# First four FFN groups begin with the two block products that need half of the tokens; output tiles written as their sums are complete

## The chip, the cores and the metric
One core of a Trainium2 chip runs one transformer block. The time is the device time of one execution in microseconds (us). The kernel before takes 2693.76 us, the median of 3 runs (2691.06 to 2694.64). One further execution was profiled: 2691.3 us, with a span of 2689.6 us from its first to its last instruction.

## The reference
The block has 512 tokens of width 2048, all in float32. Two attention branches are added to x; then the FFN follows, and it is the part that the change touches:

```
x  = x + gt1 * (merged @ w_out)
h2 = _rms(x, g_norm2) * (1 + sc2) + sh2          # the norm needs a token's whole row
gate, up = jnp.split(h2 @ w_ffn_in, 2, axis=-1)  # 2048 -> 2 x 5632
x  = x + gt2 * ((jax.nn.silu(gate) * up) @ w_ffn_out)
```

## The kernel before
**Engines.** TensorE (PE) multiplies and transposes, ScalarE (ACT) casts and applies functions, VectorE (DVE) adds and scales, SP issues the loads from memory in program order, and GpSimd (POOL) issues the stores to scratch memory and most of the output. Channels lie on the 128 partitions, tokens along the free axis.

**Three products for one.** float32 is multiplied as three products of a rounded high part and a low part: hi x lo, hi x hi, lo x hi. So each weight block is loaded raw (`raw`, 512 KB), ACT casts it to `whi`, and DVE subtracts to make `wlo`. Inputs are split in the same way (`x`, `x12h`, `x12l`).

**Seven block products.** The FFN's first matrix is worked through in 11 groups (FG) of 4 + 4 tiles of 128 columns. Within a group the product is a 2 x 2 block product: tokens in two halves (th = 0, 1), the 2048 input channels in two halves, columns in two (gate and up). Instead of 8 block products a Strassen–Winograd scheme makes 7, from sums of blocks: P1, P5, P7, P3, P6, P2, P4 in this order (lines from 1168, `PROD`). P1 is X11·W11 and P2 is X12·W21: both need the first half of the tokens alone. P5, P7, P3 and P6 need sums over both halves (`x12`, `x34`, made in `x_sums`), P4 the second half. A product is 4 pieces of 12 matmuls (128x512), 48 in all. A piece takes one weight block, or, where the scheme wants a difference of weights, a block into which DVE has subtracted another (`raw<-raw,raw`).

**Pieces and buffers.** `ahead_to(i, 2, 6)` keeps the pieces made (whi, wlo) 2 ahead and their loads issued 6 ahead; there are 10 raw buffers, 3 of whi and 3 of wlo. A block is dropped after the last product that uses it (`LAST`). PSUM has 3 buffers of the tag mm, 2 of s, 2 of t and 1 of y; P1 and P2 sum into s, s; P5 and P3 into t, t; P7 and P4 into mm, mm; P6 into mm, y. PE works in program order here, DVE and ACT in the order of a scheduler.

**Norm.** `norm2(k, th)` scales and shifts channel tile k for one half of the tokens, and splits it. It needs that half's rstd: `last_sum(th)` makes it from the sum of squares and puts it on a diagonal (`diag`), `last_row(th)` spreads it by a matmul. The first half's k < 8 are made first; then P1 of group 0 runs, with `last_sum(1)` and `last_row(1)` in it; all that remains (`second_norms`: first half's k ≥ 8, second half, sums) is issued at piece 3 of group 0, before P5.

**After the products.** `act_back1` and `act_back2` transpose a group's result back on PE, split it and park it in scratch memory by POOL's queue (`apark`). `act_back2(g-1)` runs after P1 of group g.

**FFN output and end.** The second matrix goes in 5 chunks of groups (CH), each for 2 column halves q, with the same seven products, summed in SBUF (`acc`). After P4 of the last chunk, `out_tiles(q, col_)` (lines 1470 to 1487) loads the residual (`xo<-xpark`), transposes the sums in PSUM tiles of tags mm and y, scales and adds on DVE and stores the tile; column half 1 first, then 0.

Of the kernel before, what the change touches and what calls it, by code (L numbers as in the profile page):

```python
# [9 lines left out]
F32 = mybir.dt.float32  # L10
# [77 lines left out]
def kernel(  # L88
# [40 lines left out]
    def t2(name, dtype=F32, w=T):  # L129
        return tp.tile([P, w], dtype, tag="t2", name=nm(name))  # L130
# [46 lines left out]
    def sync_dma(dst, src):  # L177
        tc.keep_in_program_order(nc.sync.dma_start(dst, src))
# [982 lines left out]
    def kmc(key, ap):  # L1161
# [6 lines left out]
    PROD = {  # L1168
        "P1": ((1, 1), "11", None), "P5": (1, "12", "11"), "P7": (3, "22", "12"), "P3": (4, "22", None),
        "P6": (2, "22", "11"), "P2": ((1, 2), "21", None), "P4": ((2, 2), "21", "22"),  # L1170
    }

    INTO = {"P5": "11", "P7": "12", "P6": "22", "P4": "21"}
    LAST = {"P7": ("12",), "P6": ("11",), "P4": ("21", "22")}

    def piece_keys(stage, g, prod, j):
        _, x, y = PROD[prod]
# [28 lines left out]
    def add_do(fn):  # L1206
        ev.append((None, fn))
# [32 lines left out]
        return [ps(t) for t in tags]  # L1240


    def ffn_in_group(g, order):
        G = {}
        n = KD // 4

        def product(prod, bank, start, stop):
            def use(w, j):
                if j == 0 and start:
                    G[bank] = tb(*{"A": ("s", "s"), "B": ("t", "t"), "C": ("mm", "mm"), "D": ("mm", "y")}[bank])  # L1250
                for kk in range(2):
                    prod_mm(G[bank], X[PROD[prod][0], 2 * j + kk], w, kk, start and j == 0 and kk == 0,
                            stop and j == n - 1 and kk == 1)
            for j in range(n):
                add_piece(("a", g, prod, j), lambda w, j=j: use(w, j))

        def both(fn):
            add_do(lambda: [fn(t) for t in range(2)])

        def copy_to(name, bank):  # L1260
            def fn(t):
                G[name, t] = t2(name)
                act.copy(G[name, t], G[bank][t])
            both(fn)

        def add_bank(name, bank, out=None):
            def fn(t):
                dst = G[name, t] if out is None else t2(out)
                vec.tensor_tensor(dst, G[name, t], G[bank][t], ALU.add)
                G[out or name, t] = dst  # L1270
            both(fn)

        def after_p6(t):
            u, z = G["u", t], G["z", t]
            vec.tensor_tensor(z, z, u, ALU.add)
            c12 = t2("c12")
            vec.tensor_tensor(c12, u, G["B"][t], ALU.add)
            G["c12", t] = c12

        def after_p2(t):  # L1280
            s = t2("silu")
            act.activation(s, G["A"][t], AF.Silu)
            vec.tensor_tensor(s, s, G["c12", t], ALU.mult)
            G["a1", t] = s
            G["c12", t] = None

        def after_p4(t):
            u = G["u", t]
            vec.tensor_tensor(u, u, G["C"][t], ALU.add)
            act.activation(u, u, AF.Silu)  # L1290
            vec.tensor_tensor(u, u, G["z", t], ALU.mult)
            G["a2", t] = u
            G["z", t] = None

        product("P1", "A", True, False)
        copy_to("p1", "A")
        if g > 0:
            add_do(lambda: act_back2(g - 1))
        product("P5", "B", True, False)
        copy_to("z", "B")  # L1300
        product("P7", "C", True, False)
        add_bank("z", "C")
        product("P3", "B", False, True)
        product("P6", "D", True, True)

        def u_of(t):
            vec.tensor_tensor(G["p1", t], G["p1", t], G["D"][t], ALU.add)
            G["u", t] = G.pop(("p1", t))
        both(u_of)
        both(after_p6)  # L1310
        product("P2", "A", False, True)
        both(after_p2)
        product("P4", "C", False, True)
        both(after_p4)
        add_do(lambda: act_back1(g))
        groups[g] = G

    groups = {}
    apark = [dp.tile([P, 7 * T], F32, name=f"apark_{i}") for i in range(2 * FG)]
    yraw = {}  # L1320

# [45 lines left out]
            park(2 * g + j, 5, split_t(s34, "y34"))  # L1367


    def first_norms():  # L1370
        for k in range(8):
            norm2(k, 0)
    add_do(first_norms)
    ffn_in_group(0, None)

    def at_product(n, fn):

        i = next(i for i, e in enumerate(ev) if e[0] == n)
# [5 lines left out]
    def second_norms():
        for k in range(8):
            norm2(k + 8, 0)
            norm2(k, 1)
            norm2(k + 8, 1)
            x_sums(k)
    at_product(3, second_norms)  # L1390
    for g in range(1, FG):
        ffn_in_group(g, None)


    CH = ((0, 1, 2), (3, 4), (5, 6), (7, 8), (9, 10))
# [17 lines left out]
    def ffn_out_chunk(ci, q):  # L1413
        B = {}
        gs = CH[ci]
        final = ci == len(CH) - 1

        def evac(prod):
            for t in range(2):
                bank = B[BANK[prod]][t]  # L1420
                if ci == 0:
                    a = t2("acc")
                    act.copy(a, bank)
                    acc[q, prod, t] = a
                else:
                    a = acc[q, prod, t]
                    vec.tensor_tensor(a, a, bank, ALU.add)
                if final:
                    finish(q, prod, t)

        for prod in ORDER:
            start = prod in ("P1", "P5", "P7", "P6")
            if ci == 0 and q == 0:
                add_do(lambda prod=prod: y_load(0, prod))
            for gi, g in enumerate(gs):
                def use(w, prod=prod, gi=gi, g=g, start=start):
                    b = BANK[prod]
                    if gi == 0 and start:
                        B[b] = tb(*TAGS[b])
                    for kk in range(2):  # L1440
                        y = Y[g, kk, prod]
                        prod_mm(B[b], (y[:, 0:256], y[:, 256:512]), w, kk, start and gi == 0 and kk == 0,
                                gi == len(gs) - 1 and kk == 1)
                        if q == 1:
                            del Y[g, kk, prod]
                add_piece(("b", (q, g), prod, 0), use)
            add_do(lambda prod=prod: evac(prod))
            if prod == "P1" and ci == q == 0:
                add_do(lambda: act_back2(FG - 1))
            if q == 1 and ci + 1 < len(CH):  # L1450
                add_do(lambda prod=prod: y_load(ci + 1, prod))

    def finish(q, prod, t):
        get = lambda n: acc[q, n, t]
        if prod == "P6":
            u = get("P6")
            vec.tensor_tensor(u, u, get("P1"), ALU.add)
            z = get("P5")
            vec.tensor_tensor(z, z, get("P7"), ALU.add)
            vec.tensor_tensor(z, z, u, ALU.add)  # L1460
            c12 = get("P3")
            vec.tensor_tensor(c12, c12, u, ALU.add)
            fin[q, 2, 2, t], fin[q, 1, 2, t] = z, c12
        if prod == "P2":
            fin[q, 1, 1, t] = get("P2")
        if prod == "P4":
            c = get("P4")
            vec.tensor_tensor(c, c, get("P6"), ALU.add)
            fin[q, 2, 1, t] = c

    def out_tiles(q, col_):
        xr_ = {}
# [24 lines left out]

# [95 lines left out]
```

## Time and profile before

| | us |
|---|---|
| median of 3 runs | 2693.76 (2691.06 to 2694.64) |
| profiled execution, its own time | 2691.3 |
| its span | 2689.6 |
| PE, DVE, ACT, POOL busy | 2584.3, 2024.8, 1149.4, 154.9 |
| mean granted PE clock | 0.985 of full speed |

Busy time counts what an engine executes, without waiting. A stretch of the span is read in a table of windows: its length, then for each engine the busy time and how many instructions it ran, then the granted clock of PE (1.00 is 2.4 GHz, half of it is 1.2 GHz), the share of time in which the DMA engines were busy, and what they moved. A group of instructions is read as: engine, operation, output<-inputs, shapes, number | busy time, mean ns of one | idle time just before, and what ended it. Names such as `ps_t` are the program's tiles without their numbers. Line L82 is that of a helper which records nearly all operations, so tiles tell more than lines.

### The profile page before, as it was taken

Reading aid. Unit: us, or ns where it says so; the run is one execution under the profiler, and the core shown is the slowest. Engines: PE = TensorE matmul, PEld = TensorE weight load, DVE = VectorE, ACT = ScalarE, POOL = GpSimd, SP = SyncE. Lnnn points to the kernel's source line nnn. Section 1 sums busy time; section 2 is a strip of 40 time slices with the busy share of each in tenths; the row PEclk is TensorE's granted clock in tenths of the full one; section 3 lists DMA queues with packets and bytes.
Section 4 is the critical chain, followed back from the end, with each engine's and each line's share of the span. In section 5 each row is a group of like instructions: output and inputs, shape, how many; then the busy total and the mean of one; then the engine's idle time right before and its main releaser. Section 6 shows DMA issues by size and latency. Waiting matters only on the chain.

```text
span 2689.6 us, 32101 instructions
## 1 busy us (share of the span) xinstructions
PE 2584.3 (96%) x12166; PEld 2147.2 (80%) x12166; DVE 2024.8 (75%) x2614; ACT 1149.4 (43%) x1557; POOL 154.9 (6%) x256
## 2 busy tenths in 40 slices
PE   6999999999999999999779999999999999999997
PEld 4788888888899888888558888888888887888885
DVE  8966766657877854533768888888888887689997
ACT  4434655542333322222545544455544445543331
POOL 0000000000110100000001100111110111000001
PEclk9999999999999999999879999999999999999998
DMA  9854444336666783332325445445444549765562
GB/s 341 300 195 164 160 150 143 128 134 235 252 248 251 263 347 141 141 141 98 94 63 167 144 136 160 158 144 172 151 136 151 164 135 327 235 210 193 189 206 79
DMA packets 236579, 487.29 MB, mean 181 GB/s; under 512 B 15428, under 2 KB 159044, under 8 KB 211336
## 3 DMA queue, kind: packets, MB, share of 16 engines
q1 hardware_dynamic: 215552, 426.03, 46.5%
q0 software_dynamic: 14816, 48.51, 5.0%
q10 hardware_dynamic: 6056, 10.70, 1.0%
q8 instruction: 95, 1.56, 0.2%
q14 instruction: 60, 0.49, 0.1%
HBM read 425.93 MB, written 59.24 MB: 180 GB/s over the span
## 4 chain that ended last, share of the span: by engine, by line
PE 71%; issue 17%; DVE 6%; DMA 3%; ACT 2%; POOL 0%; SPq 0%; POOLq 0%; ACTq 0%; DVEq 0%
PE ps_mm L82 48%; PE ps_s L82 11%; PE ps_t L82 8%; PE ps_y L82 5%; DMA raw<-in_w_ff_dram 2%; DVE wlo L82 2%; DVE raw L271 1%; ACT whi L82 1%; DVE s L82 0%; DVE raw L82 0%; DMA gpark<-sg 0%; DMA raw<-in_w_ada_dram 0%; POOL out_dram L1487 0%; DVE x L82 0%; DVE xr L82 0%
## 5 line engine op out<-in xcount | busy, mean ns | idle before, releaser
L82 ACT CAST whi<-raw 128x1024 fp32r<-128x1024 f32 x672 | 702.8, 1050 | 1037.7 <-PE ps_mm L82 471.6
L82 DVE TENSOR_TENSOR wlo<-raw,whi 128x1024 fp32r<-128x1024 f32 x672 | 815.7, 1218 | 341.2 <-ACT whi L82 338.5
L82 DVE TENSOR_TENSOR raw<-raw,raw 128x1024 f32<-128x1024 f32 x264 | 319.2, 1220 | 20.9 <-DMA raw<-in_w_ff_dram 17.7
L82 PE MATMUL ps_mm<-hl,whi 128*128 128x512 f32 x832 | 327.2, 393 | 0.0
L82 PE MATMUL ps_mm<-hh,whi 128*128 128x512 f32 x832 | 325.0, 391 | 0.0
L82 PE MATMUL ps_mm<-hh,wlo 128*128 128x512 f32 x832 | 324.9, 390 | 0.0
L271 DVE CUSTOM_DVE_ANT_0 raw<-raw,cb,cols 128x2048 f32<-128x2048 f32 x96 | 224.5, 2344 | 0.7 <-DMA raw<-in_w_ada_dram 0.7
L82 PE MATMUL ps_s<-whi,x 128*128 128x512 f32 x704 | 218.6, 392 | 0.1
L82 PEld LDWEIGHTS ps_mm<-hh,wlo 128*128 128x128 f32 x832 | 156.2, 188 | 32.7
L82 PEld LDWEIGHTS ps_mm<-hl,whi 128*128 128x128 f32 x832 | 156.6, 188 | 30.4
L82 PEld LDWEIGHTS ps_mm<-hh,whi 128*128 128x128 f32 x832 | 156.4, 188 | 30.5
L82 PEld LDWEIGHTS ps_s<-whi,x 128*128 128x128 f32 x704 | 133.3, 189 | 28.1 <-DVE x L82 0.6
L82 PE MATMUL ps_s<-wlo,x 128*128 128x512 f32 x352 | 139.3, 396 | 1.8 <-ACT x L82 1.8
L82 PE MATMUL ps_mm<-whi,yb 128*128 128x512 f32 x440 | 137.0, 393 | 0.0
L82 PE MATMUL ps_s<-whi,yb 128*128 128x512 f32 x352 | 108.5, 389 | 0.0
L82 PE MATMUL ps_t<-whi,yb 128*128 128x512 f32 x352 | 108.5, 389 | 0.0
L82 PE MATMUL ps_mm<-whi,x 128*128 128x512 f32 x352 | 108.4, 389 | 0.0
L82 PE MATMUL ps_t<-wlo,x12h 128*128 128x512 f32 x176 | 74.0, 421 | 30.5 <-ACT x12h L82 30.5
L82 PE MATMUL ps_mm<-mgl,whi 128*128 128x512 f32 (+1 forms) x272 | 102.7, 377 | 0.0
L82 PE MATMUL ps_mm<-mgh,whi 128*128 128x512 f32 (+1 forms) x272 | 102.4, 377 | 0.0
L82 PE MATMUL ps_mm<-mgh,wlo 128*128 128x512 f32 (+1 forms) x272 | 102.4, 377 | 0.0
L82 PEld LDWEIGHTS ps_mm<-whi,yb 128*128 128x128 f32 x440 | 83.5, 190 | 17.5
(363 smaller groups left out, 5147.6 us busy)
## 6 DMA issues: line engine op xcount, KB each, us to landing
raw<-in_w_ff_dram SPq DMA_DIRECT2D x264, 512.0 KB, 5.4
raw<-in_w_ada_dram SPq DMA_DIRECT2D x96, 1024.0 KB, 5.1
yb<-apark SPq DMA_DIRECT2D x154, 256.0 KB, 5.7
raw<-in_w_gate_dram SPq DMA_DIRECT2D x27, 1024.0 KB, 4.9
raw<-in_w_sb_dram SPq DMA_DIRECT2D x24, 1024.0 KB, 4.9
raw<-in_w_out_dram SPq DMA_DIRECT2D x16, 1024.0 KB, 4.8
raw<-in_w_gate_dram SPq DMA_DIRECT2D x24, 512.0 KB, 4.9
raw<-in_w_lat_dram SPq DMA_DIRECT2D x8, 1024.0 KB, 8.2
```

Source lines behind the costliest of these rows:

```text
L82: ins = f(*a, **kw)
L271: tc.keep_in_program_order(nc.vector.tensor_tensor_reduce(raw, raw, cb, 1.0, col(C_B + 16 * ADA[name] + j), ALU.mult, ALU.add, dst))
```

## The change
For groups 0 to 3 (NPRE = 4) the products P1 and P2 run at the front, under the names E1 and E2, in the order E1 of groups 0, 1, E2 of 0, 1, E1 of 2, 3, E2 of 2, 3: 32 pieces, in banks s, s and t, t by turns. `out` copies E1's result to `p1` and takes the Silu of E2's sum to `s1` on ACT; those of group 0 stay in SBUF, those of groups 1 to 3 are stored to scratch memory (`epark`, 12 stores by POOL's queue) and loaded again by SP, p1 ahead of P5, s1 after P6. The blocks W11 and W21 of these groups are dropped after the early products and loaded again for the later ones: 32 more loads of 512 KB. The number of matmuls is the same. The first half's norms of k ≥ 8 are issued at pieces 3 to 6, and `second_norms(k)` for one k at piece 7 + 3k. In groups 1 to 3 `act_back2(g-1)` stands after P5.

At the end the residual is loaded after P5 and P6 of the last chunk. After P2 come the tiles of column half 1 and the first half (256 tokens) of those of column half 0; after P4 the other half of the latter. Scalings and stores are made by halves there.

```
+    def ffn_in_early(g, i):
+        G = groups.setdefault(g, {})
+        prod = ("E1", "E2")[i]
+        for j in range(KD // 4):
+            def use(w, j=j):
+                if i == j == 0:
+                    G["A"] = tb(*(("s", "s"), ("t", "t"))[g % 2])
+                for kk in range(2):
+                    prod_mm(G["A"], X[PROD[prod][0], 2 * j + kk], w, kk, i == 0 and j == 0 and kk == 0,
+                            i == 1 and j == KD // 4 - 1 and kk == 1)
+            add_piece(("a", g, prod, j), use)
+        def out():
+            for t in range(2):
+                x = t2(("p1", "s1")[i])
+                act.activation(x, G["A"][t], (AF.Copy, AF.Silu)[i])
+                if g > 0:
+                    nc.gpsimd.dma_start(epark[g, i, t], x)
+                else:
+                    G[("p1", "s1")[i], t] = x
+        add_do(out)
...
-        product("P1", "A", True, False)
-        copy_to("p1", "A")
-        if g > 0:
+        if early and g > 0:
+            add_do(lambda: fetch_early("p1"))
+        elif not early:
+            product("P1", "A", True, False)
+            copy_to("p1", "A")
+        if g > 0 and not early:
             add_do(lambda: act_back2(g - 1))
         product("P5", "B", True, False)
         copy_to("z", "B")
+        if g > 0 and early:
+            add_do(lambda: act_back2(g - 1))
...
-        product("P2", "A", False, True)
+        if not early:
+            product("P2", "A", False, True)
+        elif g > 0:
+            add_do(lambda: fetch_early("s1"))
         both(after_p2)
...
-    ffn_in_group(0, None)
+    for g in range(0, NPRE, 2):
+        for i in range(2):
+            ffn_in_early(g, i)
+            ffn_in_early(g + 1, i)
+    for g in range(FG):
+        ffn_in_group(g, g < NPRE)
...
-    at_product(3, second_norms)
+    for k in range(8):
+        at_product(3 + k // 2, lambda k=k: norm2(k + 8, 0))
+        at_product(7 + 3 * k, lambda k=k: second_norms(k))
...
+            if final and prod == "P5":
+                add_do(lambda: out_load(q, 1))
+            if final and prod == "P6":
+                add_do(lambda: out_load(q, 0))
+            if final and prod == "P2":
+                add_do(lambda: out_tiles(q, 1, (0, 1)))
+                add_do(lambda: out_tiles(q, 0, (0,)))
+            if final and prod == "P4":
+                add_do(lambda: out_tiles(q, 0, (1,)))
...
-    def out_tiles(q, col_):
+    def out_tiles(q, col_, rows):
...
+            vec.scalar_tensor_tensor(xr[:, cs], o[:, cs], ada["gt2"][:, m:m + 1], xr[:, cs], ALU.mult, ALU.add)
+            (nc.gpsimd if q == 0 or rows[-1] == 0 else nc.sync).dma_start(outT[m * P:(m + 1) * P, cs], xr[:, cs])
```

The places below show instructions in the order of their engine; a row has the helper's line, the operation, output<-inputs with the tiles' numbers, the output's shape, and how many of the kind follow each other.

On PE, at the end of group 0's first product (ps_s) before: P5 (ps_t) follows, and needs x12h.

```order
L82 MATMUL ps_s_10795<-wlo_10828,x_10776 128x512
L82 MATMUL ps_s_10795<-whi_10827,x_10776 128x512 x2
...
L82 MATMUL ps_t_11103<-wlo_10850,x12h_10881 128x512
L82 MATMUL ps_t_11103<-whi_10849,x12h_10881 128x512
L82 MATMUL ps_t_11103<-whi_10849,x12l_10882 128x512
L82 MATMUL ps_t_11104<-wlo_10850,x12h_10881 128x512
```

The same place of the changed kernel, where the t bank is that of E1 of group 1.

```order
L83 MATMUL ps_s_10807<-wlo_10840,x_10788 128x512
L83 MATMUL ps_s_10807<-whi_10839,x_10788 128x512 x2
...
L83 MATMUL ps_t_10924<-wlo_10861,x_10753 128x512
L83 MATMUL ps_t_10924<-whi_10860,x_10753 128x512 x2
L83 MATMUL ps_t_10925<-wlo_10861,x_10753 128x512
L83 MATMUL ps_t_10925<-whi_10860,x_10753 128x512 x2
```

The product that follows reads `x` tiles of the first half; P5 now comes 28 pieces later.

On DVE, in the second half's norms before (xr are the tiles of x, s and x12l belong to `x_sums`):

```order
L82 SCALAR_TENSOR_TENSOR x_10873<-xr_10128,ada_sh_183,x_10873 128x256
L82 SCALAR_TENSOR_TENSOR xr_9732<-xr_9732,ada_gs_182,rstd_10596 128x256
L82 SCALAR_TENSOR_TENSOR xr_10260<-xr_10260,ada_gs_182,rstd_10596 128x256
L82 TENSOR_TENSOR s_1889_10877<-xr_9601,xr_10128 128x256
L82 SCALAR_TENSOR_TENSOR xr_9798<-xr_9798,ada_gs_182,rstd_10596 128x256
L82 TENSOR_TENSOR s_1889_10877<-s_1889_10877,xr_9601 128x256
```

The changed kernel's DVE around the first of these sums:

```order
L83 SCALAR_TENSOR_TENSOR x_10997<-xr_10140,ada_sh_183,x_10997 128x256
L83 TENSOR_TENSOR wlo_11018<-raw_1889_10886,whi_11017 128x1024
L83 TENSOR_TENSOR s_1912_11001<-xr_9613,xr_10140 128x256
L83 TENSOR_TENSOR s_1912_11001<-s_1912_11001,xr_9613 128x256
L83 TENSOR_TENSOR wlo_11042<-raw_1896_10918,whi_11041 128x1024
L83 TENSOR_TENSOR x12l_11006<-s_1912_11001,x12h_11005 128x512
```

A weight's `wlo` now stands between the steps of one tile's norm and sums.

On PE, from the end of P2 of the last chunk and the second q (ps_s), before:

```order
L82 MATMUL ps_s_20916<-wlo_21081,yb_20510 128x512
L82 MATMUL ps_s_20916<-whi_21080,yb_20510 128x512 x2
L82 MATMUL ps_mm_20992<-wlo_21108,yb_20550 128x512
...
L82 MATMUL ps_mm_20993<-whi_21124,yb_20556 128x512 x2
L82 MATMUL ps_mm_21178<-consts,acc_18560 128x128
L82 MATMUL ps_mm_21178<-consts,acc_18562 128x128
```

And of the changed kernel (a row that reads `consts` is a transpose):

```order
L83 MATMUL ps_s_21040<-wlo_21213,yb_20622 128x512
L83 MATMUL ps_s_21040<-whi_21212,yb_20622 128x512 x2
L83 MATMUL ps_mm_21284<-consts,acc_18672 128x128
...
L83 MATMUL ps_y_21327<-consts,acc_18805 128x128
L83 MATMUL ps_mm_21124<-wlo_21250,yb_20662 128x512
...
L83 MATMUL ps_mm_21125<-whi_21266,yb_20668 128x512 x2
L83 MATMUL ps_mm_21358<-consts,acc_18870 128x128
```

24 of the 32 transposes stand between P2 and P4 now, and 8 after P4.

## Rows read from the trace of the kernel before

**Rows 1.** The page: busy time by engine, and the 40 slices.
```profile
PE 2584.3 (96%) x12166; PEld 2147.2 (80%) x12166; DVE 2024.8 (75%) x2614; ACT 1149.4 (43%) x1557; POOL 154.9 (6%) x256
...
PE   6999999999999999999779999999999999999997
...
PEclk9999999999999999999879999999999999999998
```

**Rows 2.** Windows: stretch, length, busy PE PEld DVE ACT POOL, clock, DMA share, GB/s.
```profile
1304.40:1326.36 21.96, 15.21 (x56) 11.69 (x55) 21.43 (x52) 15.65 (x33) 0.54 (x1) 0.84 0.02 6
1326.36:1391.05 64.69, 34.23 (x97) 23.22 (x96) 47.86 (x83) 32.69 (x58) 0.00 (x0) 0.63 0.11 33
1391.05:1412.81 21.76, 21.76 (x97) 18.02 (x96) 15.54 (x15) 8.45 (x8) 0.00 (x0) 1.00 0.33 98
1595.23:1674.62 79.39, 78.32 (x354) 64.62 (x353) 65.70 (x74) 39.44 (x49) 9.68 (x14) 1.00 0.49 153
1674.62:1754.08 79.46, 78.36 (x353) 64.56 (x353) 67.67 (x76) 39.74 (x49) 9.66 (x14) 1.00 0.48 153
2615.20:2629.99 14.79, 11.66 (x60) 8.95 (x58) 13.85 (x18) 2.95 (x3) 3.26 (x6) 0.90 0.55 186
2629.99:2663.20 33.21, 33.21 (x146) 27.05 (x144) 32.21 (x38) 11.61 (x11) 1.09 (x3) 0.99 0.08 29
2663.20:2689.60 26.40, 11.57 (x57) 8.86 (x56) 12.09 (x17) 1.05 (x1) 3.24 (x6) 0.72 0.33 119
```

**Rows 3.** Chain of waits, a product in a later group: start, us, what.
```profile
1630.22 10.88 PE ps_t L82 x48
```

**Rows 4.** Waits of PE, 1304 to 1391 us: total us, times, longest.
```profile
PE ps_t L82 <- ACT x12h L82: 30.5, 7, 5.9
PE ps_y L82 <- DVE diag L82: 4.8, 1, 4.8
```

**Rows 5.** Groups of instructions, 1304 to 1391 us, DVE and ACT.
```profile
L82 DVE SCALAR_TENSOR_TENSOR xr<-xr,ada_gs,rstd 128x256 f32<-128x256 f32 x30 | 13.4, 477 | 0.0
L82 DVE TENSOR_TENSOR x12l<-s,x12h 128x512 fp32r<-128x512 f32 x8 | 5.5, 689 | 3.8 <-ACT x12h L82 3.8
L82 DVE TENSOR_TENSOR s<-xr,xr 128x256 f32<-128x256 f32 x8 | 3.4, 421 | 2.9 <-ACT xr L82 2.9
...
L82 ACT CAST whi<-raw 128x1024 fp32r<-128x1024 f32 x12 | 12.5, 1044 | 9.8 <-PE ps_mm L82 5.8 <-PE ps_t L82 2.9 <-DVE raw L82 0.5
L82 ACT ACTIVATE x<-xr,ada_sh 128x256 fp32r<-128x256 f32 x24 | 10.7, 498 | 0.0
L82 ACT COPY p<-ps_s 128x512 f32<-128x512 f32 x2 | 1.1, 583 | 0.0
```

**Rows 6.** Groups of instructions of DVE in one later group, 1595.23 to 1674.62 us.
```profile
L82 DVE TENSOR_TENSOR wlo<-raw,whi 128x1024 fp32r<-128x1024 f32 x28 | 34.0, 1221 | 11.1 <-ACT whi L82 11.0
L82 DVE TENSOR_TENSOR raw<-raw,raw 128x1024 f32<-128x1024 f32 x16 | 19.3, 1218 | 2.6 <-DMA raw<-in_w_ff_dram 2.4
```

**Rows 7.** Timeline of DVE in that group: start, us, what, idle before.
```profile
1619.38 1.23 DVE L82 TENSOR_TENSOR raw<-raw,raw 128x1024 f32<-128x1024 f32 x1 [1.14 <-DMA raw<-in_w_ff_dram]
```

**Rows 8.** Timeline at the two ends, and one scaling of half size.
```profile
1304.57 0.48 DVE L82 SCALAR_TENSOR_TENSOR xr<-ps_mm,ada_gt,xr 128x256 f32<-128x256 f32 x1
...
2629.99 0.74 PE L82 MATMUL ps_s<-wlo,yb 128*128 128x512 f32 x1
...
2669.51 1.38 DVE L82 TENSOR_TENSOR acc<-acc,ps_mm 128x512 f32<-128x512 f32 x2 [2.45 <-PE ps_mm L82]
2670.00 0.60 PE L82 MATMUL ps_mm<-consts,acc 128*128 128x128 f32 x4
2674.97 1.12 PE L82 MATMUL ps_y<-consts,acc 128*128 128x128 f32 x4 [0.41 <-DVE xo L82]
2678.73 0.75 DVE L82 SCALAR_TENSOR_TENSOR xo<-ps_mm,ada_gt,xo 128x512 f32<-128x512 f32 x1 [3.82 <-DMA xo<-xpark]
2681.93 0.75 DVE L82 SCALAR_TENSOR_TENSOR xo<-ps_y,ada_gt,xo 128x512 f32<-128x512 f32 x1 [0.54 <-PE ps_y L82]
```

More of the change, by code (lines that the diff above doesn't have):

```diff
@@ L35 @@
 GF = (1, 1)
+NPRE = 4
 C_B = 0
@@ L1170 @@
         "P6": (2, "22", "11"), "P2": ((1, 2), "21", None), "P4": ((2, 2), "21", "22"),
[1 row of a table added]
     }
     INTO = {"P5": "11", "P7": "12", "P6": "22", "P4": "21"}
-    LAST = {"P7": ("12",), "P6": ("11",), "P4": ("21", "22")}
+    LAST = {"P7": ("12",), "P6": ("11",), "P4": ("21", "22"), "E1": ("11",), "E2": ("21",)}
     def piece_keys(stage, g, prod, j):
@@ L1240, in tb, with ffn_in_group, fetch_early @@
         return [ps(t) for t in tags]
-    def ffn_in_group(g, order):
-        G = {}
+    def ffn_in_early(g, i):
[18 more added lines that the diff above has]
+        add_do(out)
+    def ffn_in_group(g, early):
+        G = groups.setdefault(g, {})
         n = KD // 4
+        def fetch_early(name):
+            for t in range(2):
+                G[name, t] = t2(name)
+                sync_dma(G[name, t], epark[g, ("p1", "s1").index(name), t])
         def product(prod, bank, start, stop):
@@ L1280, in after_p2 @@
         def after_p2(t):
-            s = t2("silu")
-            act.activation(s, G["A"][t], AF.Silu)
+            if early:
+                s = G.pop(("s1", t))
+            else:
+                s = t2("silu")
+                act.activation(s, G["A"][t], AF.Silu)
             vec.tensor_tensor(s, s, G["c12", t], ALU.mult)
@@ L1315, in ffn_in_group @@
         add_do(lambda: act_back1(g))
-        groups[g] = G
     groups = {}
+    epark = {(g, i, t): dp.tile([P, T], F32, name=f"epark_{g}_{i}_{t}")
+             for g in range(1, NPRE) for i in range(2) for t in range(2)}
     apark = [dp.tile([P, 7 * T], F32, name=f"apark_{i}") for i in range(2 * FG)]
@@ L1379, in at_product, with second_norms @@
         ev.insert(i, (None, fn))
+    def second_norms(k):
+        norm2(k, 1)
+        norm2(k + 8, 1)
+        x_sums(k)
     at_product(1, lambda: last_sum(1))
     at_product(2, lambda: last_row(1))
[L1384 to L1389, printed above, removed]
-    at_product(3, second_norms)
-    for g in range(1, FG):
-        ffn_in_group(g, None)
+    for k in range(8):
+        at_product(3 + k // 2, lambda k=k: norm2(k + 8, 0))
+        at_product(7 + 3 * k, lambda k=k: second_norms(k))
     CH = ((0, 1, 2), (3, 4), (5, 6), (7, 8), (9, 10))
@@ L1463, in finish @@
             fin[q, 2, 2, t], fin[q, 1, 2, t] = z, c12
+            c = get("P4")
+            vec.tensor_tensor(c, c, u, ALU.add)
         if prod == "P2":
@@ L1466, in finish, with out_load @@
         if prod == "P4":
-            c = get("P4")
-            vec.tensor_tensor(c, c, get("P6"), ALU.add)
-            fin[q, 2, 1, t] = c
-    def out_tiles(q, col_):
-        xr_ = {}
+            fin[q, 2, 1, t] = get("P4")
+    xres = {}
+    def out_load(q, col_):
         for i in range(4):
             m = 4 * (2 * q + col_) + i
-            xr = t2("xo")
-            sync_dma(xr, xpark[m])
-            xr_[i] = xr
+            xres[m] = t2("xo")
+            sync_dma(xres[m], xpark[m])
+    def out_tiles(q, col_, rows):
         for i in range(4):
@@ L1480, in out_tiles @@
             o = ps(("mm", "y")[i % 2])
-            for r in range(2):
+            for r in rows:
                 for t in range(2):
@@ L1484, in out_tiles @@
                                  fin[q, r + 1, col_ + 1, t][:, i * P:(i + 1) * P], ident)
-            xr = xr_[i]
-            vec.scalar_tensor_tensor(xr, o, ada["gt2"][:, m:m + 1], xr, ALU.mult, ALU.add)
-            (nc.gpsimd if m < 14 else nc.sync).dma_start(outT[m * P:(m + 1) * P, :], xr)
+            xr = xres[m]
+            cs = slice(256 * rows[0], 256 * rows[-1] + 256)
+            vec.scalar_tensor_tensor(xr[:, cs], o[:, cs], ada["gt2"][:, m:m + 1], xr[:, cs], ALU.mult, ALU.add)
+            (nc.gpsimd if q == 0 or rows[-1] == 0 else nc.sync).dma_start(outT[m * P:(m + 1) * P, cs], xr[:, cs])
     for ci in range(len(CH)):
@@ L1491 @@
             ffn_out_chunk(ci, q)
-            if ci == len(CH) - 1:
-                for col_ in (1, 0):
-                    add_do(lambda q=q, col_=col_: out_tiles(q, col_))
     run_steps()
```

1 row of the table PROD is left out of this document.

## The prediction
> **What bounds the kernel now.** I read the page's busy times first: TensorE is busy for 96% of the span, VectorE for 75%, and the slices show where the missing 4% lies: PE falls to 7 tenths in slices 20 and 21, and the granted clock falls to 8 and 7 there [rows 1]. So nearly all of the time is matmuls at full clock, and only a stage in which PE stands still, or a removed matmul, can move the total. The change removes no matmul: what moves is the stage around 1304 to 1391 us and the end.
>
> I then read that place by stretches [rows 2]. From 1326.36 to 1391.05 us PE runs the FFN's products P5 and P7 of group 0, 96 matmuls. In a later group one product of 48 takes 10.88 us [rows 3], and the next stretch, also 96 matmuls, takes 21.76 us at a granted clock of 1.00 [rows 2]. So 64.69 − 21.76 = 42.9 us are lost, at a granted clock of 0.63. The waits name the cause: PE waits 30.5 us in 7 waits for ACT's x12h, and 4.8 us for diag in the stretch before [rows 4]. DVE is busy for 47.86 of the 64.69 us, ACT for 32.69 [rows 2]: the two work in turns on the norms and the sums of the second half, while PE has nothing that doesn't need them. The remaining 42.9 − 30.5 = 12.4 us are matmuls run below full clock.
>
> In the later groups PE is busy for 78.3 of 79.4 us and the clock is 1.00; DVE is busy for 65.70 and 67.67 us [rows 2]. A group is bound by PE, and DVE has some 12.8 us of slack in it.
>
> **Part A, the early products.** P1 and P2 of groups 0 to 3 become 8 products at the front, 8 x 10.88 = 87 us of PE work that needs only the first half. The 42.9 us of loss now has PE work beside it, so nearly all of it can go. What is late next:
> - VectorE. From piece 7 on, three pieces (8.16 us of PE) bring three wlo (3 x 1.22 = 3.66) [rows 6] and one second_norms: 3 scalings of 0.477, 4 sums of 0.42, two splits of 0.69, together 4.48 [rows 5]. That is 8.14 us of DVE for 8.16 us of PE, no slack. Pieces 3 to 6 have 1.22 + 4 x 0.477 = 3.1 against 2.72. The first two pieces of P5, made ahead, add a subtraction each (2 x 1.22). I charge the phase 3 us.
> - ScalarE. A piece behind the evacuation (2 copies of 0.583) and two norms of about 1.0 (two activations) waits 1.2 + 2.0 + 1.04 for its whi [rows 5], then 1.22 for wlo: 5.4 us against two pieces in hand. I charge 1 us.
> - P5 of group 0 wants the t banks that the last early product leaves, behind two Silu, at a copy's 0.583: 1 us.
> So 5 us, from 2 (only the bank and one piece) to 12 (3 us, and 30 pieces each 0.3 us late). Gain 42.9 − 5 = 38 us, from 31 to 41. The 4.8 us for diag and the first stretch's clock of 0.84 [rows 2, 4] stand before the new products and stay.
>
> The 32 added loads of 512 KB fall into these 87 us: 193 GB/s; the late stretch with the most traffic here moved 186 GB/s at a DMA share of 0.55 [rows 2]. I charge nothing; should the cover fail, it shows as waits for raw, and I keep that in the range's upper end.
>
> **Part B, groups 0 to 3 without P1 and P2.** Their 20 remaining pieces need 79.42 − 21.76 = 57.7 us of PE. DVE loses 8 wlo, 9.8 us [rows 6], so it has 66.7 − 9.8 = 56.9 us for 57.7: 98 to 99% busy, where it had 84%. A group has 28 wlo and 16 subtractions, all in 28 pieces [rows 6]; the 16 stay. In the trace PE loses about 1.1 us per group even now [rows 2], and one subtraction stands idle 1.14 us for its load [rows 7], because P7's third block takes the buffer that P7's first frees. With DVE later by some us the buffers come free later too. Lowest cost 0 (DVE just keeps pace); highest 15: the 2.7 us of one whole piece late in each group, 11, and 4 for a lower clock after it. Nearest row: the 1.1 us per group of now; I take 4. The 12 parks and 12 fetches (256 KB each) ride on POOL's and SP's queues, which are nearly empty in the stage (9.7 us of POOL busy per group [rows 2]); an SP fetch of p1 is queued between raw loads, one transfer of half a load: nothing.
>
> **Part C, the end.** Before, P4 of the last chunk (24 matmuls, 5.44 us) comes first, then all 8 output tiles, and P1 of the second q starts at 2629.99: 14.79 us after 2615.20 [rows 2, 8]. Now four whole tiles and four half ones come before P4, with one mm and one y buffer between PE and DVE, since P4's mm pair is still summing. Four transposes took 0.60 to 1.12 us; I take 0.66, and 0.4 for two. With two buffers a tile costs half of its transposes and scaling, (0.66 + 0.74) / 2 = 0.70, a half one (0.4 + 0.48) / 2 = 0.44 [rows 8]. Sum for q = 0: P2's adds 1.38 and 0.5 until the first transposes; 4 x 0.70 + 4 x 0.44 = 4.6; P4 5.44 and 2 for matmuls below full clock; P4's adds, now nothing beside them, 1.9; 4 x 0.44 = 1.8; and two wlo that DVE does between, 2. That is 19.6 against 14.8: 5 us lost. For q = 1: before, the last scaling ends at 2682.68, 19.48 after 2663.20; of it 3.82 is a wait for the xo load that now is issued earlier [rows 8]. Now 1.9 + 4.6 + 7.4 + 1.9 + 1.8 + 0.5 and one wlo of 1.22, 19.3: no gain. After the last scaling 6.92 us follow for the store; the last stores are half as large, I leave it. Tail: −5, from +1 (scalings hide wholly, the wait for xo goes) to −12.4 (below).
>
> A row bears on P4's clock: the transposes before 2629.99 were followed by a first matmul of 0.74 us and then by a stretch of 146 matmuls in 33.21 us at 0.99; the stage with the transposes had 0.90, and the last one 0.72 [rows 2, 8]. So the clock of 2.4 GHz was there again within a few matmuls. The Trainium skill (TensorE: Matmul & The Clock Gate, "Part 4: PE-mode transpose") states that transposes don't count as busy in the way of matmuls and that the full clock isn't engaged by them. By that rule P4 would run whole at 1.2 GHz, 5.44 us more in each q where I charge 2, and the tail would be 6.9 us worse; the row speaks against it for 9 us of transposes, and no row shows them ahead of so short a product.
>
> **The sum.** 38 − 4 − 5 = 29 us of gain. The profiled execution took 2691.3 us with a span of 2689.6, so 2662.3 of its own time. The median of the three runs, 2693.76, lies 2.46 above it: 2664.8, and I say 2665. The ends: 41 − 0 + 1 = 42 gives 2651.8; 31 − 15 − 12.4 = 4 gives 2690.
>
> **The rivals.**
> 1. DVE keeps pace and the tail costs nothing: 41 − 2 − 0 = 39, 2655. For it: pieces are made two ahead, and the scheduler may place norms in gaps. Against it: 98 to 100% of DVE in two phases leaves no gap [rows 2, 5, 6]. 25%.
> 2. VectorE becomes the bound in both phases: front 8 lost (35 gained), groups 15, tail 5: 15 gained, 2679. For it: the same 98%, and a raw buffer that returns late. Against it: the average is still under PE's need. 20%.
> 3. Slower: PE's clock. In the stretch with waits for DVE and ACT the 96 matmuls were granted 0.63 and took 34.23 us of busy time for 21.76 of work, 1.57 times [rows 2]. If DVE's lateness in groups 0 to 3 leaves so many short holes that a group of 57.7 us runs at that level, it costs 33 us; one such group takes the whole gain (29 − 33 = −4, 2698). [...] Against it: a slower PE wants fewer pieces from DVE, so the holes close by themselves. 6%.
> 4. The change does nothing that can be measured: rivals 2 and half of 3's clock cancel the gain. 4%.
> The forecast has 45%.
>
> **How the numbers follow.** A difference under 0.2%, 5.4 us, can't be told from none here. Faster by more than that: forecast, rivals 1 and 2, 90%; the same: 4%; slower: 6%. The range of 8 in 10 runs from 2649 (rival 1 with all it can have and 3 for the runs' scatter) to 2683 (rival 2 with a tail of 9); above it lie rivals 3 and 4 and the worst of 2.
>
> **What would show it.** Right: the stretch between the last out-projection matmuls and P5 of group 0 is 87 us of PE with few holes at a clock near 1.00, waits for x12h under 3 us, P5 and P7 of group 0 in 22 to 25 us, DVE over 95% busy. Groups 1 to 3 take 58 to 60 us each (wrong if over 62). From P2's end to the second q's first matmul about 19 to 20 us, and about 26 from P2's end to the span's end in q = 1. The forecast is wrong in its main step if PE still waits over 10 us for x12h, and wrong in its sizes if DVE waits show up in groups 0 to 3 with over 4 us each, or if the tail is no longer than before.

## The result and the profile after

The changed kernel takes 2664.61 us (median of 4 runs, 2663.69 to 2668.23); the kernel before, beside it, 2693.25. The ratio is 0.9897, with a 95% interval of 0.988 to 0.9914: 28.6 us faster, where 2665, a gain of 29, was forecast. The profiled execution took 2668.23 us with a span of 2666.5; it is the slowest of the four, so some 3.6 us in its trace belong to that execution and not to the change.

The page of the changed kernel, busy times and slices, shows the dip of [rows 1] gone: slices 20 and 21 of PE hold 8 and 9, and the granted clock 9.

```profile
PE 2582.4 (97%) x12166; PEld 2145.6 (80%) x12166; DVE 2023.5 (76%) x2622; ACT 1147.9 (43%) x1557; POOL 162.9 (6%) x270
...
PE   6999999999999999999899999999999999999998
...
PEclk9999999999999999999999999999999999999998
```

Stretches of the changed kernel follow, with the columns of [rows 2]. The first five run from the first early product to the end of group 0 (P5 begins at 1407.31, P3 at 1429.83), three more are groups 1 to 3, and the last two go from P2 of a column half's last chunk to the next q's first product, and to the span's end.

```profile
1308.21:1319.68 11.47, 6.96 (x31) 5.37 (x31) 11.47 (x32) 8.73 (x20) 0.00 (x0) 0.93 0.33 97
1319.68:1382.23 62.55, 62.55 (x267) 51.50 (x266) 50.12 (x81) 46.84 (x76) 3.23 (x6) 0.96 0.63 194
1382.23:1407.31 25.08, 22.74 (x97) 17.60 (x95) 23.05 (x34) 16.24 (x25) 2.15 (x4) 1.00 0.69 213
1407.31:1429.83 22.52, 22.23 (x97) 18.05 (x98) 15.31 (x14) 9.82 (x11) 1.07 (x2) 1.00 0.36 110
1429.83:1462.94 33.11, 32.93 (x145) 26.91 (x144) 32.86 (x35) 12.66 (x12) 0.00 (x0) 1.00 0.64 196
1462.94:1520.87 57.93, 56.87 (x257) 46.48 (x256) 53.65 (x65) 29.37 (x36) 9.72 (x14) 1.00 0.71 224
1520.87:1582.21 61.34, 57.42 (x257) 46.39 (x256) 57.55 (x67) 29.47 (x36) 9.70 (x14) 1.00 0.67 217
1582.21:1642.90 60.69, 57.16 (x257) 46.47 (x256) 54.94 (x65) 29.35 (x36) 9.70 (x14) 1.00 0.67 217
2581.42:2608.03 26.61, 19.65 (x81) 14.74 (x80) 23.14 (x33) 5.14 (x5) 4.71 (x9) 0.81 0.40 138
2636.94:2666.50 29.56, 19.49 (x81) 14.53 (x79) 18.24 (x29) 2.10 (x2) 2.16 (x4) 0.77 0.20 71
```

P5 and P7 of group 0 take 22.52 us where they took 64.69 [rows 2], and PE is busy through the second stretch without a hole. The last two stretches answer to these of before:

```profile
2610.05:2629.99 19.94, 16.81 (x82) 13.23 (x80) 19.00 (x26) 4.01 (x4) 3.26 (x6) 0.93 0.51 170
2657.61:2689.60 31.99, 17.16 (x81) 13.18 (x79) 17.68 (x25) 2.10 (x2) 3.24 (x6) 0.77 0.27 98
```

PE's waits in the changed kernel from 1319.7 to 1430 us, and from 1425 to 1720 (total us, times, longest): no wait for x12h is left.

```profile
PE ps_y L83 <- DVE diag L83: 4.5, 1, 4.5
PE ps_s L83 <- DVE wlo L83: 1.4, 1, 1.4
PE ps_t L83 <- ACT s L83: 0.9, 1, 0.9
```
```profile
PE ps_t L83 <- DVE wlo L83: 5.4, 6, 1.5
PE ps_mm L83 <- DVE wlo L83: 4.7, 6, 1.3
```

Cut at the same program points, and with 10.88 us for each product that stands on another side of a cut, the two spans differ so:

| stretch | before | after | gain |
|---|---|---|---|
| start to the first product | 1306.31 | 1308.21 | −1.9 |
| first product to P3 of group 0 (7 products more after) | 84.74 | 121.62 − 76.16 | +39.3 |
| P3 of group 0 to the end of group 3 (7 fewer) | 283.33 | 213.86 + 76.16 | −6.7 |
| group 4 to P2 of the last chunk, q = 0 | 935.67 | 937.73 | −2.1 |
| that P2 to the next q's first product | 19.94 | 26.61 | −6.7 |
| to P2 of q = 1 | 27.62 | 28.91 | −1.3 |
| to the span's end | 31.99 | 29.56 | +2.4 |
| sum | 2689.6 | 2666.5 | +23.1 |

The first and fourth rows, 4.0 us, lie where the change touches nothing. Such differences come with the execution: in the traces of the kernels below the first product starts between 1306.4 and 1309.3 us. So one trace doesn't tell where this execution lost its 3.6 us.

### The profile page after: what moved, and what is told of

Same layout as the page of the kernel before. It is cut to its first block, busy times and chain, and to the rows that moved or that the text cites. A ratio compares the mean times of both kernels' runs of the same rounds, so it can differ in the third digit from the quotient of the medians.

```text
span 2666.5 us, 32303 instructions
## 1 busy us (share of the span) xinstructions
PE 2582.4 (97%) x12166; PEld 2145.6 (80%) x12166; DVE 2023.5 (76%) x2622; ACT 1147.9 (43%) x1557; POOL 162.9 (6%) x270
## 4 chain that ended last, share of the span: by engine, by line
PE 74%; issue 15%; DVE 6%; DMA 3%; POOL 1%; ACT 1%; SPq 0%; POOLq 0%; ACTq 0%; DVEq 0%
PE ps_mm L83 47%; PE ps_s L83 11%; PE ps_t L83 10%; PE ps_y L83 5%; DVE wlo L83 2%; DMA raw<-in_w_ff_dram 1%; DVE raw L272 1%; POOL apark L1370 1%; ACT whi L83 1%; DVE acc L83 1%; DVE raw L83 1%; DMA gpark<-sg 0%; DMA raw<-in_w_ada_dram 0%; DVE s L83 0%; DMA apark<-y34h 0%
## 5 line engine op out<-in xcount | busy, mean ns | idle before, releaser
L83 PE MATMUL ps_s<-whi,x 128*128 128x512 f32 x576 | 179.2, 393 | 0.0
L83 PEld LDWEIGHTS ps_s<-whi,x 128*128 128x128 f32 x576 | 109.3, 190 | 22.8 <-DVE x L83 0.2
L83 PE MATMUL ps_s<-wlo,x 128*128 128x512 f32 x288 | 114.4, 397 | 3.9 <-DVE wlo L83 2.1
L83 PE MATMUL ps_mm<-wlo,yb 128*128 128x512 f32 x220 | 88.3, 401 | 5.7 <-DVE wlo L83 5.7
```

Source lines behind the costliest of these rows:

```text
L83: ins = f(*a, **kw)
```

## The experiments

**The two halves of the change alone.** `early_only` has the early products with the end of the kernel before; `tail_only` the new end alone.

```
early_only: - out_load / out_tiles after P5, P6, P2, P4      tail_only: NPRE, E1, E2 and the norms' places
            + all out_tiles after P4, as before                         as before
```

> The early products with the end of the kernel before. My theory: the gain comes from the front alone, less about 7 us in groups 0 to 3, and the new end costs some 5 to 6 us; so 2659 us here (5.5 below the changed kernel), with 32 us gained between the first product and the end of group 3. Rival: the end is neutral and the front gives just the 28 us measured; then 2664 to 2665.

> The kernel before with the new end alone. My theory: slower than before by 5 to 6 us, 2698.5: about 6.7 lost at q = 0 between P2 and the next q's first product, 1.3 in the products behind it, 2.4 won back at the very end by the shorter last store. Rival: the new end is neutral or better, 2690 to 2694.

Measured: `early_only` 2660.33 us (2654.0 to 2661.98), ratio 0.9873 (0.9859 to 0.9886), 4.3 us less than the changed kernel. `tail_only` 2695.93 us (2692.83 to 2697.62) beside 2693.12, ratio 1.0008 (0.9999 to 1.0017). So the front gives all of the gain, and by these medians the end takes 2.8 or 4.3 us of it, less than the 5 to 6 that I expected. `tail_only` by itself isn't told apart from the kernel before, since its interval reaches 0.9999. In the trace of `tail_only` the stretch from P2 to the next q's first product takes 25.3 us, 5.4 more than before, and the last stretch 29.1, 2.9 less.

**How much cover the front needs.** `npre2` and `npre6` move 2 and 6 groups, with the second half's norms spread over the shorter or longer phase.

```
- NPRE = 4                                      + NPRE = 2          + NPRE = 6
- at_product(7 + 3 * k, ...second_norms(k))     + at_product(7 + k) + at_product(7 + 5 * k)
```

> NPRE = 2 with second_norms(k) at piece 7 + k: 16 early pieces, 43.5 us of cover. My theory: the norms and sums need some 65 us of VectorE beside the pieces' own, so P5 of group 0 starts about 75 us after the first product and TensorE waits 15 to 20 us for x12h; groups 2 and 3 win back 6 us: 2676 to 2680. Rival: the gain comes from issuing the norms spread among products rather than from the length of the cover; then the front loses nothing and the groups win 6: 2658 to 2660.

> NPRE = 6 with second_norms(k) at piece 7 + 5k: 48 early pieces, 131 us of cover. My theory: the front has VectorE slack now and wins back its 3 us of late pieces, while groups 4 and 5 lose 3 us each as groups 2 and 3 do: 2667 to 2668. Rival: more cover is free, so 2661 to 2662.

Measured: `npre2` 2691.86 us (2690.11 to 2693.37), ratio 0.9995 (0.9986 to 1.0004): no gain. `npre6` 2663.48 us (2659.25 to 2664.46), ratio 0.9888 (0.9874 to 0.9901): as four groups, between the two expectations. Its front wins 2.2 us more, and groups 4 and 5 take 59.6 and 59.9 us, where 57.7 of matmuls are left. For two groups both theories were too hopeful. P5 of group 0 starts at 1396.90, 87.6 us after the first product, nearly as late as with four groups (99.1), after a wait of 33.7 us. Up to P3 of group 0 the trace has a gain of 5.2 us (84.74 before; 112.17 less three products), about what the new end takes. PE's longest wait of `npre2`, ScalarE's timeline in it (start, us, what, idle before), and two stretches with the columns of [rows 2]:

```profile
PE ps_t L83 <- ACT s L83: 33.7, 1, 33.7
```
```profile
1388.41 0.62 ACT L83 CAST x12h<-s 128x512 fp32r<-128x512 f32 x1 [0.95 <-DVE s L83]
1390.46 0.62 ACT L83 CAST x34h<-s 128x512 fp32r<-128x512 f32 x1 [1.43 <-DVE s L83]
...
1393.69 0.62 ACT L83 CAST x12h<-s 128x512 fp32r<-128x512 f32 x1 [0.95 <-DVE s L83]
...
1396.26 1.08 ACT L83 ACTIVATE s<-ps_t 128x512 f32<-128x512 f32 x2
```
```profile
1341.12:1370.39 29.27, 21.31 (x93) 16.90 (x91) 26.94 (x39) 15.32 (x23) 1.07 (x2) 0.95 0.50 148
1370.39:1396.90 26.51, 0.00 (x0) 0.00 (x0) 15.17 (x32) 12.75 (x23) 0.00 (x0) 0.50 0.00 0
```

At the end one k goes around every 5.28 us (1388.41 to 1393.69): ACT and DVE hand the same tile back and forth, and neither is full, DVE busy for 15.17 and ACT for 12.75 of 26.51 us. The first three turns, up to 1370.39, take 7.6 to 10.5 us each, with DVE busy for 26.94 of 29.27 us, since weights stand between their steps. My estimate of 75 us had added up DVE's busy time, and that fits only these first turns; behind them the chain counts, which fewer pieces don't shorten.

The last row shows a second cost, the one on which PE's wait ends: the Silu that frees P5's t banks was placed behind the whole chain on ACT, though the product that it reads ended at 1363.2. The first three x12h were there by then. Without that, P5 could have followed the chain and ended soon after its last x12l (1395.0), where it ended at 1410.1; so I estimate from these rows that some 12 us hang on the Silu's place, which no run tried apart. With four groups the cover, 87 us of products, is as long as this stage (87.6 us); with two it is half.

**The wait for diag.** `row_late` moves one call.

```
-    at_product(2, lambda: last_row(1))
+    at_product(5, lambda: last_row(1))
```

> The changed kernel with last_row(1) issued at piece 5 instead of piece 2. My theory: TensorE's 4.5 us wait for diag at piece 2 is now needless, since there is other work for it, and goes: 2660. Rival: VectorE sets the length of the early phase (no slack from piece 7 on), so what is saved at piece 2 comes back as waits for wlo before P5: 2664 to 2665.

Measured: 2660.83 us (2658.96 to 2663.58), ratio 0.988 (0.9866 to 0.9893): 3.8 us less than the changed kernel, as expected. The wait for diag is gone, but part of it comes back later: before P5, PE waits 4.3 us for the Silu on ACT. From the first product to P3 of group 0 it takes 118.0 us instead of 121.6.

**What holds groups 2 and 3.** Three edits: `back2_late` and `back2_p7` move act_back2 behind P3 and behind P7; `less_dve` leaves out part of its work.

```
 product("P5"...)
-if g > 0 and early: add_do(lambda: act_back2(g - 1))
 product("P7"...); add_bank("z", "C")
+if g > 0 and early: add_do(lambda: act_back2(g - 1))     # back2_p7
 product("P3"...)
+if g > 0 and early: add_do(lambda: act_back2(g - 1))     # back2_late
```

> The changed kernel with act_back2 of the group before issued after P3 instead of after P5, in groups 1 to 3. My theory: groups 2 and 3 lose 3 us each because act_back2's work on VectorE falls on P7, whose pieces need a subtraction and a wlo each, while P3's need a wlo alone; behind P3 it costs nothing, so 5 us less than the changed kernel, 2660, and waits for wlo in the groups under 3 us. Rival: the average load of 98% sets the loss wherever the work stands; then 2664 to 2665 and 10 us of waits for wlo as now, at other products.

> The changed kernel with act_back2 of the group before issued after P7, so that its ACT copy out of the y bank has P3's 10.9 us ahead of P6, which takes that bank; behind P3 the bank cost TensorE 16.3 us. My theory (VectorE's peak in P5 and P7 sets the loss of groups 2 and 3): 2660 to 2661, the three groups at 58 us each, waits for wlo in them under 3 us. Rival (the average of 98% sets it): 2664 to 2665, and 61 us each for groups 2 and 3.

> The changed kernel with the s34 sums and their split left out of act_back2 for groups 0 to 2 (other data of the same size are parked in their place, so the stores stay): 2 x (2 x 0.42 + 0.69) = 3.1 us of VectorE and 1.2 of ScalarE less in each of groups 1 to 3. This leaves out part of the computation. My theory: groups 2 and 3 (61 us for 57.7 of matmuls) are bound by VectorE's sum of work, so they shorten by some 2.5 to 3 us each: 2659 to 2660. Rival: late buffers (the raw block that P7 needs, stores that hold the sums' tiles) bind them, not the sum of work: 2664 to 2665, 61 us each as now.

Measured: `back2_late` 2687.35 us (2683.5 to 2688.24), ratio 0.9976 (0.9966 to 0.9986). It tested something else: P6 follows at once and takes the y bank, which act_back2's copy on ACT still reads.

```profile
PE ps_y L83 <- ACT y L83: 16.3, 3, 5.7
```

`back2_p7`, without that fault, 2667.02 us (2666.28 to 2668.07), ratio 0.9904 (0.989 to 0.9918): no gain, groups 2 and 3 at 62.7 and 62.2 us. So moving the work off P5 and P7 doesn't take the loss away. `less_dve` 2663.36 us (2662.16 to 2665.0), ratio 0.9892 (0.9879 to 0.9906): groups 2 and 3 still take 60.8 and 60.7 us, so less work alone isn't it either. Its trace shows another limit, in DVE's and SP's timelines and PE's waits:

```profile
1529.29 2.48 DVE L83 TENSOR_TENSOR wlo<-raw,whi 128x1024 fp32r<-128x1024 f32 x2
...
1534.59 1.23 DVE L83 TENSOR_TENSOR raw<-raw,raw 128x1024 f32<-128x1024 f32 x1 [0.75 <-DMA raw<-in_w_ff_dram]
```
```profile
1520.52 0.84 SPq L179 DMA_DIRECT2D p<-epark  x2
1530.54 19.77 SPq L179 DMA_DIRECT2D raw<-in_w_ff_dram  x6
```
```profile
PE ps_mm L83 <- DVE wlo L83: 6.4, 4, 2.8
```

SP issues no raw load from 1515 to 1530.54: it waits for a buffer, which is free when wlo of P7's first piece is made. The blocks land 4.7 us later (median), and P7 takes 15.6 us for 10.88 of matmuls, while P5 no longer waits. In the changed kernel the same pause of the loads runs from 1516.2 to 1533.4 us. The wait that the prediction had seen once in the kernel before [rows 7] is here the one that decides.

**The end with more PSUM buffers.** `tail_banks`:

```
-  o = ps(("mm", "y")[i % 2])
+  column half 1: banks t, t, mm, y; column half 0, first rows: s, s (two half tiles in a bank),
+  between P4's two pieces; its second rows: t, t after P4; a set's transposes all before its scalings
```

> The changed kernel with the early output tiles in more PSUM buffers: column half 1 in t, t, mm, y; the first half of column half 0 in s, s, between P4's two pieces; the rest in t, t after P4. My theory: the cost of the new end is TensorE waiting for one mm and one y buffer; without that 6 to 8 us less at q = 0 and 4 to 7 us less at q = 1: 2650 to 2655. Rival: VectorE's own work (adds, wlo, scalings) or the clock after the transposes sets the end, so that the buffers change little: 2662 to 2665.

Measured: 2650.04 us (2647.23 to 2651.87), ratio 0.984 (0.9826 to 0.9853): 14.6 us less than the changed kernel, and about 10 less than the old end with the early products. The changed kernel's end at q = 1, PE and then DVE in their timelines, shows what was taken away:

```profile
2642.82 0.60 PE L83 MATMUL ps_y<-consts,acc 128*128 128x128 f32 x4
2648.15 1.12 PE L83 MATMUL ps_mm<-consts,acc 128*128 128x128 f32 x4 [4.73 <-DVE xo L83]
```
```profile
2642.67 1.22 DVE L83 TENSOR_TENSOR wlo<-raw,whi 128x1024 fp32r<-128x1024 f32 x1
2643.80 1.22 DVE L83 TENSOR_TENSOR raw<-raw,raw 128x1024 f32<-128x1024 f32 x1
2644.94 1.28 DVE L83 TENSOR_TENSOR acc<-acc,ps_s 128x512 f32<-128x512 f32 x2
2646.21 1.23 DVE L83 TENSOR_TENSOR wlo<-raw,whi 128x1024 fp32r<-128x1024 f32 x1
2647.35 0.75 DVE L83 SCALAR_TENSOR_TENSOR xo<-ps_mm,ada_gt,xo 128x512 f32<-128x512 f32 x1
```

With two buffers, PE may transpose two tiles and then stands for 4.73 us, since the first scaling is fifth in DVE's row, behind P4's own weights. In `tail_banks` the two stretches shrink from 26.61 and 29.56 us:

```profile
2580.37:2600.00 19.63, 15.47 (x81) 12.90 (x80) 19.62 (x30) 4.30 (x5) 4.34 (x8) 0.96 0.53 186
2628.13:2650.20 22.07, 15.05 (x81) 12.24 (x79) 17.55 (x29) 2.11 (x2) 2.16 (x4) 0.91 0.27 95
```

At q = 0 DVE is busy for 19.62 of 19.63 us: there VectorE is the bound, and the rival holds from that point on. The old end takes 19.1 and 30.1 us for the same two stretches in the trace of `early_only`: so the early tiles win nothing at q = 0 and 8.0 us at the span's end. The edit changed buffers, order and place together; which of them counts how much was not separated.

**Together, and two tries on the groups.** `best` joins `row_late` and `tail_banks`; `best_pool` moves four operations of each of groups 0 to 3 to GpSimd as well; `best_raw11` is `best` with one more raw buffer and one general tile less.

```
best_pool:  - vec.tensor_tensor(z, z, u, ALU.add)             + nc.gpsimd.tensor_tensor(z, z, u, ALU.add)
            - vec.tensor_tensor(s, s, G["c12", t], ALU.mult)  + nc.gpsimd.tensor_tensor(s, s, G["c12", t], ALU.mult)
best_raw11: - tile_pool(name="rp2", bufs=10)                  + bufs=11
            - tile_pool(name="tp", bufs=68)                   + bufs=67
```

> The changed kernel with two edits together: last_row(1) at piece 5, and the early output tiles in more PSUM buffers. Alone they gave 2660.8 and 2650.0 against 2664.6; they act at places far apart, so the gains should add: 2646. Rival: the runs' scatter made one of them look larger; then 2650.

> As the kernel with both edits, and in groups 0 to 3 the additions z += u and the products s *= c12 (four of 128x512 in each group) go from VectorE to GpSimd: 2.7 us of VectorE less per group. Their results are wanted only behind P4, 11 us later. My theory (VectorE's sum of work binds groups 2 and 3): 4 to 6 us less than that kernel, 2641. Rival: GpSimd is slow at them, and P4's end or act_back1 waits for it, or VectorE slows beside it: 2646 to 2650.

> The kernel with both edits, with 11 raw weight buffers instead of 10; one of the 68 general tiles is given up for the space. Taking 3.1 us of VectorE work out of each group didn't shorten it, and the loads for P7's third block are issued only when wlo of its first is made. My theory now: that late buffer, not VectorE's sum of work, binds groups 1 to 3, and costs about 1 us in groups 4 to 10 too. With one more buffer P7 of groups 2 and 3 takes 11 to 11.5 us instead of 13.5, and the whole 8 to 13 us less: 2635 to 2640. Rival: VectorE's sum binds groups 2 and 3 after all; then only groups 4 to 10 gain, P7 of groups 2 and 3 stays near 13 us, 2641 to 2643. The tile given up may cost: then slower than 2648.

Measured: `best` 2648.09 us (2647.84 to 2649.81), ratio 0.9837 (0.9823 to 0.985), 2.0 us less than `tail_banks`: the gains add but for 1.8 us. The time lies halfway between the expectation and its rival, and the two kernels' ranges overlap, so `row_late`'s gain isn't shown a second time. `best_pool` 2651.82 us (2650.49 to 2652.21), ratio 0.9848 (0.9834 to 0.9861): slower than `best`, by 5.3 us in group 1 of the trace, while groups 2 and 3 take 0.8 and 0.6 us less. `best_raw11` 2635.10 us (2632.98 to 2639.8), ratio 0.9794 (0.978 to 0.9807): 57.6 us below the kernel before beside it and 13 below `best`.

The time came out as my theory had it, but not at the place. P7 of groups 2 and 3 takes 11.0 us, as the theory said. Yet the groups take 59.8 and 60.4 us, where `best` has 62.0 and 60.6: P5 waits for wlo as before, and P3 now too. Group 2 of `best_raw11`, and PE's waits for wlo in t banks from 1300 to 1660 us:

```profile
1514.31:1574.11 59.80, 57.05 (x257) 46.42 (x256) 56.54 (x67) 29.36 (x37) 9.67 (x14) 1.00 0.68 220
```
```profile
PE ps_t L83 <- DVE wlo L83: 8.5, 8, 1.6
```

In groups 1 to 3 the buffer saves 1.1 us in all. From group 4 to P2 of the last chunk it saves 10.6 us (926.95 for 937.50), all of it in groups 4 to 10, some 1.6 us in each, and 3 us in the front. So in groups 2 and 3 two limits seem to lie close together: with less work for VectorE the late raw buffer holds the group (`less_dve`), and with one more buffer the wait for wlo does, with VectorE busy for 56.54 of 59.80 us. That VectorE's sum of work is this second limit, and that both edits together would bring the groups to 58 us, is argued, not tried.

## Why the prediction was right

**The front.** 42.9 less 5, a gain of 38, was forecast; the stretch gave 39.3. Waits for x12h are gone, P5 and P7 of group 0 take 22.5 us (22 to 25 was named). Of the 5 us charged, 3.6 came; one piece waits 1.4 us for wlo, and P5 0.9 for the Silu on the t bank; 1 us each was charged. The larger term, 3 us for VectorE, was mis-sized: VectorE was to be over 95% busy and is busy for 84.6 of 99.1 us. The durations I added are those of single instructions; in a row they start sooner than that (last section). The prediction also measured the cover needed by VectorE's load alone, while in `npre2` the turns between ACT and DVE, and a Silu behind them, hold P5 where neither engine is full. Four groups cover the stage by either reckoning.

**Groups 0 to 3.** 4 was forecast, 6.7 came, within 0 to 15. The step charged for VectorE at 98%; it is busy for 57.55 of 61.34 us in group 2. The late buffer, named there as a follower of DVE's lateness, is a limit of its own. Groups 1 to 3 took 57.93, 61.34 and 60.69 us for 58 to 60 named; PE's waits for wlo in groups 2 and 3, 3.9 and 3.5 us, stay just under the 4 us named as a sign of being wrong.

**The end.** A loss of 5 was forecast; the trace has 5.5 (6.7 + 1.3 − 2.4), the medians of the two halves 2.8 and 4.3. Three terms missed and nearly cancelled. At q = 0 it takes 21.0 us from P2's end, not 19.6, since a tile's price of 0.70 doesn't hold while the first scaling is fifth in DVE's row. The 1.3 us, matmuls of the next q below full clock, weren't in the sum. At the end I left the store's 6.92 us as they were; from the last scaling's end (2662.98) to the span's end it is 3.5. That 5.5 meets 5 is also luck of the execution: from P2 of q = 0 to the span's end eight traces with this end take 81.3 to 85.1 us, this one the longest, and the two with the old end 79.6 and 76.7. Two sums were a little off: the old end took 14.3 us from P2's end (2615.65), not 14.8 from 2615.20, and −5 − 6.9 gives −11.9 for the tail's lowest value, not −12.4.

**The total.** 28.6 us for 29 is closer than the parts, 39.3, −6.7 and −5.5 in the trace for 38, −4 and −5: their misses partly cancel, so part of the agreement is luck.

**P4's clock.** The stretches around P4 at q = 1 follow: PE's wait for the first scaling, the transposes behind it, and P4 in two parts. The last row is the same place of `tail_banks`: 16 transposes, P4's first piece, 8 transposes, its second.

```profile
2643.42:2648.15 4.73, 0.00 (x1) 0.00 (x0) 4.73 (x7) 1.04 (x1) 0.00 (x0) 0.76 0.00 0
2648.15:2652.57 4.42, 4.10 (x16) 2.79 (x17) 3.39 (x6) 0.00 (x0) 0.54 (x1) 0.50 0.64 237
2652.57:2656.37 3.80, 3.80 (x11) 2.99 (x10) 0.52 (x2) 0.00 (x0) 1.62 (x3) 0.53 0.30 105
2656.37:2660.10 3.73, 3.63 (x17) 2.69 (x15) 0.80 (x2) 0.00 (x0) 0.00 (x0) 1.00 0.10 34
```
```profile
2633.57:2641.41 7.84, 7.84 (x48) 6.87 (x47) 7.84 (x11) 1.06 (x1) 0.00 (x0) 1.00 0.16 60
```

P4's matmuls run at half pace for nearly 4 us, at a granted clock of 0.53, and at full pace behind: from its first to its last P4 takes 7.4 us here and 7.7 at q = 0, where 24 matmuls at full clock take 5.6. So the 2 us charged were right in size, but transposes alone don't bring the clock down: it fell while PE stood for 4.73 us, and in `tail_banks`, without that wait, it is 1.00 through 24 transposes and P4. The rule of the Trainium skill (TensorE: Matmul & The Clock Gate, "Part 4: PE-mode transpose") is that transposes don't engage the full clock. The trace agrees as far as the clock stayed at 0.50 through 4.42 us of transposes behind the wait. That P4 would run at 1.2 GHz as a whole, which I had made of the rule, did not happen.

**The rivals.** A gain of 39 with a free end needed the groups at 57.7 us; groups 2 and 3 weren't. VectorE as the bound in both phases needed a front that loses 8 us and groups that lose 15; they lose 3.6 and 6.7. A granted clock that falls in groups 0 to 3 is ruled out: it is 1.00 in all of them. Where PE does wait some 8 us in each group, in `back2_late`, it is 0.92 to 0.95 there, not the 0.63 that this rival priced.

## What to carry to other kernels

To hide a stage behind other work, measure how long the stage takes, and not only its engines' busy time: two engines that hand one tile back and forth are late with neither of them full, and a bank that is freed behind them is later still. Half of the cover won 5 us of the 43 here, and all of it 39. When a group stops at just its bound, taking away one limit may only show the next; take away two suspected limits together as well, which was not done here. In the end's runs, tiles put between products cost little with more PSUM buffers, and without them PE stood for 4.73 us behind the other engine's queue and then ran at half pace.

## What the runs showed of the hardware

**Short instructions in a row.** VectorE's instructions overlap a little: in the changed kernel's timeline a sum of 0.42 us is followed by the next after 0.34, and a subtraction of 1.22 after 1.13. Adding means of single instructions overstates a row of short ones by up to a fifth.

```profile
1537.21 0.42 DVE L83 TENSOR_TENSOR s<-s,y 128x256 f32<-128x256 f32 x1
1537.55 1.22 DVE L83 TENSOR_TENSOR raw<-raw,raw 128x1024 f32<-128x1024 f32 x1
1538.68 0.69 DVE L83 TENSOR_TENSOR y12l<-s,y12h 128x512 fp32r<-128x512 f32 x1
```

**GpSimd beside VectorE.** GpSimd's product of 128x512 took 2.27 us, where VectorE's takes 0.68, and VectorE's own subtractions were longer in that kernel: in each group the three that ran beside GpSimd's sums and products took 2.0 to 2.3 us. A group of POOL's instructions and two of DVE's in `best_pool` from 1460 to 1650 us, then the same two of `best`:

```profile
L1316 POOL TENSOR_TENSOR s<-s,c 128x512 f32<-128x512 f32 x6 | 13.5, 2270 | 0.0
```
```profile
L83 DVE TENSOR_TENSOR wlo<-raw,whi 128x1024 fp32r<-128x1024 f32 x64 | 84.1, 1321 | 3.6 <-ACT whi L83 3.0
L83 DVE TENSOR_TENSOR raw<-raw,raw 128x1024 f32<-128x1024 f32 x44 | 55.1, 1266 | 6.2 <-DMA raw<-in_w_ff_dram 6.2
```
```profile
L83 DVE TENSOR_TENSOR wlo<-raw,whi 128x1024 fp32r<-128x1024 f32 x63 | 76.1, 1218 | 4.1 <-ACT whi L83 3.8
L83 DVE TENSOR_TENSOR raw<-raw,raw 128x1024 f32<-128x1024 f32 x48 | 57.5, 1217 | 2.6 <-DMA raw<-in_w_ff_dram 2.6
```

Twelve operations of 0.68 us, 8.2 us, left VectorE in these three groups; 64 x 0.103 + 44 x 0.049 = 8.7 us came back in longer subtractions.

**The last store.** Why the last store ends 3.4 us sooner (halves of 128 KB, or the queues they take) was not separated.
